# Seven block products for eight: the Delta half of an output projection, by pairs of chunks

## The chip, the cores and the metric

The kernel runs on one core of a Trainium2 chip. The metric is the device time of one execution in microseconds (us), lower being better. Beside the runs' times there is one profiled execution, from which every row of a profile in this document comes.

## The reference

One layer of an encoder: RMSNorm, one input projection, two head groups that read it (a bidirectional gated DeltaNet of 4 heads of 128, and windowed attention of 8 heads of 64), and one output projection of both groups' outputs, added to the input. Cut to what matters here, with S = 2048 rows and D = 1024 columns:

```python
dn = dn * jax.nn.silu(dn_z)          # (2048, 512): 4 heads x 128
sw = sw * jax.nn.silu(sw_z)          # (2048, 512)
mix = jnp.concatenate([dn, sw], axis=-1)
x = x + mix @ w_out                  # w_out: (1024, 1024)
```

The "Delta half" of the output is `dn @ w_out[:512]`.

## The kernel before, in words

The rows are 16 chunks of 128. Phase A (`phase_a`) normalises, projects and computes the attention group; phase B (`phase_b`) does the delta rule for one head after the other, and the output projection in two halves. The TensorE (PE) multiplies float32 numbers in the type float32r, with each operand split into a high part (a copy to float32r by ScalarE, ACT) and a low part (the rest, by VectorE, DVE); a product is then three matmuls: high x high, low x high, high x low.

*Per head* phase B does `pre_front` (Gram matrices of a chunk, with decays, into tiles `ma`, L703), `solve` and `invert` (the inverse of a triangular block, tiles `pi`, L772) and `scan` (L798): 16 steps forward and 16 backward, each a chain of small matmuls (pk, py, po), DVE updates (r, S) and ACT copies (y, yk). `post` (L855) is called at step 12 for the groups of chunks 4 to 11 and after the last step for the others: it takes squares (jko) and a power on GpSimd (POOL, sso), scales, transposes (tro), multiplies by the gate (zt) and stores to `mix_dn` in DRAM (L882). The scan of one head overlaps the preparation of the next; heads alternate between two pools of tiles, hd0 (heads 0 and 2) and hd1 (heads 1 and 3). Pool kx holds half of head 2's ks and vs.

*The attention half of the output* is 32 units (`sw_units`, L567; a chunk and 512 columns each; tiles mxs, mhs, mls, pcs) that add their product to the input rows (xrs) and store partial rows `part` in DRAM (L603). They fill PE during scans; their staging tiles are in pool swp, their PSUM banks are those of ps_t and ps_g.

*The Delta half* is what the change touches. `load_wo` (L537) loads w_out[:512] as eight pieces of 128x512 and splits each (L545, L546) into pool op; then `out_dn` (L919) is called for the chunks in the order 7, 8, 6, 9, ... 0, 15. It loads 128 rows of `mix_dn` as one 128x512 tile mxd (L922), splits it (mhd L553, mld L554), and `out_half` (L549) computes for each of two halves of the columns 4 x 3 matmuls into a bank pcd (L561 to L563), adds the partial row xrd (loaded by L558, added by L564) and stores it (L565). The chunks 4 to 11 can go ahead once head 3's scan has passed step 12; the others wait for its end.

*Pools.* hd0 and rp, hd1, swp, kx stand on two sides of SBUF. q1, qa, qb (of `pre_front`, `solve` and `invert`), kx, swp and the PSUM pools ps_t, ps_g, ps_i are released together (`pre_stack.close()`, L913); op and ps_c (L914, L915) then take space that they had.

*The order of the work* is not that of the program. `set_order` (L938) builds the graph of all instructions, gives each a cost (L1091; a DMA also a fixed 2.4 us until it lands, L931), plans forward and backward with queues per engine (`plan`, L1174), keeps the plan with the earliest end, and fixes it as the order of each engine and of the DMA queue on SP. In this graph a pool that lies where released pools were waits as a whole: all users of the old pools come before all users of the new one (`behind`, L1045, L1071). Instructions of DVE and POOL with two inputs in SBUF are planned one at a time (L1145, L1215). At run time an instruction waits only for the tiles that it uses, but in this order.

Of the kernel before, what the change touches and what calls it, by code (L numbers as in the profile page):

```python
# [7 lines left out]
F32 = mybir.dt.float32  # L8
F32R = mybir.dt.float32r
AF = mybir.ActivationFunctionType  # L10
ALU = mybir.AluOpType
AX = mybir.AxisListType
PSUM = bass.MemoryType.PSUM
DRAM = bass.MemoryType.DRAM

P = 128
S = 2048
D = 1024
# [4 lines left out]
NQ = 8  # L23
EPS = 1e-6
NDEC = 1
SCRATCH = 1024
NEG = -1e30
FILLF = ((0, 0, 0, 8), (0, 0, 0, 8), (0, 0, 0, 8))
# [4 lines left out]
def tile_hybrid(ctx, tc, t, out, dbg=None):  # L33
# [26 lines left out]
    with ExitStack() as cb, ExitStack() as wide:  # L60
        with ExitStack() as ca:
            consts, late = phase_a(ca, wide, tc, t, ident, nw, bd, gp, mix_sw, kq_d, v_d, zdn_d, zsw_d, dp)
        phase_b(cb, wide, late, tc, t, ident, consts, hp, mix_dn, mix_sw, kq_d, v_d, zdn_d, zsw_d, dp, out)
# [367 lines left out]
def delta_setup(tc, t, ident, bd, gp, ap, bp, pj, q_pool):  # L431
# [71 lines left out]
    dec_d = {}  # L503
    for h in range(NDEC):
        for d in range(2):
# [14 lines left out]
def phase_b(ctx, wide, late, tc, t, ident, consts, hp, mix_dn, mix_sw, kq_d, v_d, zdn_d, zsw_d, dp, out):  # L520
    nc = tc.nc
    V, A, G, T = nc.vector, nc.scalar, nc.gpsimd, nc.tensor
    dma = nc.sync.dma_start

    def pool(name, bufs=1, stack=ctx, **kw):
        return stack.enter_context(tc.tile_pool(name=name, bufs=bufs, reuse_waits="tile", **kw))
# [7 lines left out]

    part_d = [dp.tile([P, D], F32, tag=f"part{c}", name=f"part{c}") for c in range(NCH)]

    def load_wo(pool, k0, name, tg=""):  # L537
        wh = pool.tile([P, 4, D], F32R, tag="woh" + tg, name=f"woh{name}", bufs=1)
        wl = pool.tile([P, 4, D], F32R, tag="wol" + tg, name=f"wol{name}", bufs=1)
        for k in range(4):  # L540
            for j in range(2):
                ns = slice(j * 512, (j + 1) * 512)
                sw = pool.tile([P, 512], F32, tag="ws", name=f"wos{name}_{k}_{j}")
                dma(sw, t["wout"][:, k0 + k, ns])
                A.activation(wh[:, k, ns], sw, AF.Copy)  # L545
                V.tensor_tensor(wl[:, k, ns], sw, wh[:, k, ns].bitcast(F32), ALU.subtract)  # L546
        return wh, wl

    def out_half(pool, bank, w, mx, src, dst, name, nb):  # L549
        wh, wl = w  # L550
        mh = pool.tile([P, 4, P], F32R, tag="mh", name=f"mh{name}", bufs=nb)
        ml = pool.tile([P, 4, P], F32R, tag="ml", name=f"ml{name}", bufs=nb)
        A.activation(mh, mx, AF.Copy)  # L553
        V.tensor_tensor(ml, mx, mh.bitcast(F32), ALU.subtract)  # L554
        for j in range(2):
            ns = slice(j * 512, (j + 1) * 512)
            xr = pool.tile([P, 512], F32, tag="ws", name=f"xr{name}_{j}")
            dma(xr, src[:, ns])  # L558
            ps = bank(j, f"pc{name}_{j}")
            for k in range(4):  # L560
                T.matmul(ps, mh[:, k], wh[:, k, ns], start=(k == 0), stop=False)  # L561
                T.matmul(ps, ml[:, k], wh[:, k, ns], start=False, stop=False)  # L562
                T.matmul(ps, mh[:, k], wl[:, k, ns], start=False, stop=(k == 3))  # L563
            V.tensor_tensor(xr, xr, ps, ALU.add)  # L564
            dma(dst[:, ns], xr)  # L565

    def sw_units(pool):  # L567
        w = {}

# [44 lines left out]
    ORD = (7, 8, 6, 9, 5, 10, 4, 11, 3, 12, 2, 13, 1, 14, 0, 15)  # L614
    pre_stack = ctx.enter_context(ExitStack())
    hd = [pool("hd0")]
    q1 = pool("q1", stack=pre_stack)
    qa = pool("qa", stack=pre_stack)
    qb = pool("qb", stack=pre_stack)
    ps_i = [pool("ps_i0", stack=pre_stack, space=PSUM), pool("ps_i1", stack=pre_stack, space=PSUM)]  # L620
# [16 lines left out]
    def pre_front(h):  # L637
# [12 lines left out]
        for n, c4 in enumerate(FRONT):  # L650
# [7 lines left out]
            for d in range(2):  # L658
                gm = q1.tile([P, 4, P], F32, tag="gm", name=f"dc{h}_{c4}_{d}", bufs=4)
                if h < NDEC:  # L660
                    dma(gm.rearrange("p c i -> p (c i)"), dec_d[h, d][c4])
# [28 lines left out]
            for c2 in range(2):  # L690
# [6 lines left out]
                for k in range(2):  # L697
                    c = 2 * c2 + k
                    cc = 4 * c4 + c
                    for d in range(2):  # L700
                        if h >= NDEC:
                            A.activation(gms[d][:, c], gms[d][:, c], AF.Exp, bias=ngc[:, d, cc, h : h + 1])
# [181 lines left out]
    def bank(k):  # L884
        return lambda nm: (ps_t, ps_g, ps_i[0], ps_i[1])[k].tile([P, 512], F32, tag=("tr", "gh", "inv", "inv")[k], name=nm)
# [13 lines left out]
    with tc.using_default_side("right"):  # L899
# [3 lines left out]
        kx = pool("kx", stack=pre_stack)  # L903
# [6 lines left out]
        invert(h + 1, H)  # L910
    for k in range(32):
        fill(1, bank(k % 2))
    pre_stack.close()  # L913
    op = pool("op", 4)  # L914
    ps_c = pool("ps_c", 4, space=PSUM)  # L915
    with tc.high_priority(-1000000):
        w = load_wo(op, 0, "d")

    def out_dn(c):  # L919
        sc = slice(c * P, (c + 1) * P)  # L920
        mx = op.tile([P, 4, P], F32, tag="mx", name=f"mxd{c}", bufs=2)
        dma(mx, mix_dn[:, :, sc].rearrange("f p s -> p f s"))  # L922
        out_half(op, lambda j, nm: ps_c.tile([P, 512], F32, tag="pc", name=nm), w, mx, part_d[c], out[sc, :], f"d{c}", 2)

    scan(3, H)
    for c in ORD:
        out_dn(c)


ENGINES = ("PE", "DVE", "Activation", "Pool", "SP")  # L930
# [3 lines left out]

SBUF_BYTES = 229344 - SCRATCH - 128

# [372 lines left out]
```

## Time and profile before

| | |
|---|---|
| median of 3 runs | 1280.27 us |
| lowest, highest | 1278.16, 1280.57 us |
| the profiled execution | 1274.25 us |
| its span, first to last instruction | 1272.5 us |
| mean granted PE clock | 0.992 |
| matmuls of the Delta half (pcd) | 384, from 1175.5 us of the span on |
| matmuls of the attention half (pcs) | 384, from 808.1 to 1171.4 us |
| DMA queue of hardware, whole span | 203.92 MB, 52.7% of 16 engines |

Rows of a profile name a line of the kernel (L561), an engine (PE matmuls, PEld weight loads, DVE, ACT, POOL, SPq the DMA queue), an operation, tiles without their numbers (out<-in), and a count (x48). "idle before <- releaser" is time that the engine sat idle, and what ended it. Matmuls are pipelined: the duration of one is longer than the distance to the next. A row of stretches gives from:to, the length, then busy time and count of PE, PEld, DVE, ACT, POOL, then the granted PE clock (1 is full), the DMA engines' busy share, and GB/s.

### The profile page before, as it was taken

How to read it: one execution, taken by the hardware profiler on the slowest of the kernel's cores; microseconds unless marked ns; L12 is line 12 of the kernel's file. 1: busy time of each engine (PE TensorE's matmuls, PEld its weight loads, DVE VectorE, ACT ScalarE, POOL GpSimd, SP SyncE). 2: the span in 40 equal slices, each digit the busy share in tenths (PEclk: the TensorE clock that was granted, in tenths of full speed). 3: DMA queues.
4: the chain of work that ended last, by engine and by line, in shares of the span. 5: the costliest groups of instructions: out<-in, count | busy, mean ns of one | idle time of the engine just before them, and what ended most of it. 6: DMA issues, size and time to landing. Idle time of an engine off the chain costs nothing.

```text
span 1272.5 us, 22253 instructions
## 1 busy us (share of the span) xinstructions
PE 1219.4 (96%) x7066; PEld 1044.4 (82%) x7066; DVE 889.5 (70%) x2154; ACT 703.2 (55%) x2105; POOL 507.4 (40%) x893
## 2 busy tenths in 40 slices
PE   6999999999999999999999998998799899999998
PEld 6998877788889998787788787887688789798876
DVE  4422387999975589999986573788488879557333
ACT  6321254776644677776654425858557955566210
POOL 1330044666613398665221306613672651641000
PEclk9999999999999999999999998999899999999999
DMA  8442254322544434522137826967965974746675
GB/s 269 145 132 76 95 180 128 97 97 81 180 132 144 130 96 116 158 87 67 58 117 244 224 96 189 276 189 207 270 169 154 269 191 138 217 145 214 227 242 205
DMA packets 225510, 205.34 MB, mean 161 GB/s; under 512 B 48497, under 2 KB 175089, under 8 KB 225393
## 3 DMA queue, kind: packets, MB, share of 16 engines
q1 hardware_dynamic: 225392, 203.92, 52.7%
q8 instruction: 56, 0.92, 0.3%
q14 instruction: 62, 0.50, 0.1%
HBM read 138.79 MB, written 65.08 MB: 160 GB/s over the span
## 4 chain that ended last, share of the span: by engine, by line
PE 67%; DVE 12%; DMA 9%; ACT 7%; issue 3%; POOL 1%; SPq 0%; DVEq 0%; ACTq 0%; POOLq 0%
PE pf_c L191 4%; PE pf_c L192 4%; PE pf_c L193 4%; PE pf_z L191 4%; PE pf_z L192 4%; PE pf_z L193 4%; PE pi L772 4%; DVE acc L242 3%; PE pt L363 3%; PE pq_q L202 2%; PE pq_q L204 2%; PE pq_q L203 2%; PE pcd L561 2%; PE pcd L563 2%; PE pcd L562 2%
## 5 line engine op out<-in xcount | busy, mean ns | idle before, releaser
L191 PE MATMUL pf_c<-xhi,wh_c 128*128 128x512 f32 x384 | 151.0, 404 | 0.7 <-DVE acc L242 0.4
L192 PE MATMUL pf_c<-xlo,wh_c 128*128 128x512 f32 x384 | 150.6, 401 | 0.0
L193 PE MATMUL pf_c<-xhi,wl_c 128*128 128x512 f32 x384 | 149.1, 401 | 0.0
L242 DVE SCALAR_TENSOR_TENSOR acc<-pf_c,cw,acc 128x512 f32<-128x512 f32 (+1 forms) x192 | 140.3, 743 | 11.3 <-ACT acc L238 9.2
L358 POOL TENSOR_SCALAR pr<-pr,st 128x384 f32<-128x384 f32 (+1 forms) x128 | 80.1, 648 | 71.3 <-DVE st L356 60.0
L191 PE MATMUL pf_z<-xhi,wh_z 128*128 128x512 f32 x256 | 86.6, 401 | 0.5 <-DVE zo L215 0.5
L349 ACT ACTIVATE pr<-pr,st 128x384 f32<-128x384 f32 (+1 forms) x128 | 76.1, 596 | 19.6 <-DVE st L345 19.1
L192 PE MATMUL pf_z<-xlo,wh_z 128*128 128x512 f32 x256 | 86.2, 399 | 0.0
L191 PEld LDWEIGHTS pf_c<-xhi,wh_c 128*128 128x128 f32 x384 | 72.1, 188 | 15.3 <-DVE acc L242 1.7
L193 PE MATMUL pf_z<-xhi,wl_z 128*128 128x512 f32 x256 | 84.7, 397 | 0.0
L192 PEld LDWEIGHTS pf_c<-xlo,wh_c 128*128 128x128 f32 x384 | 72.3, 188 | 13.0
L193 PEld LDWEIGHTS pf_c<-xhi,wl_c 128*128 128x128 f32 x384 | 71.8, 188 | 13.0
L345 DVE CUSTOM_DVE_ANT_0 pr<-s,mask,sink 128x384 f32<-128x384 f32 (+1 forms) x128 | 72.5, 593 | 12.4 <-PE s L344 8.3
L367 ACT ACTIVATE ph<-pt 128x512 fp32r<-128x512 f32 x92 | 53.0, 596 | 40.9 <-PE pt L363 39.1
L826 ACT ACTIVATE yk<-py,ck 128x128 f32<-128x128 f32 x120 | 43.9, 366 | 49.5 <-PE py L821 48.4
L363 PE MATMUL pt<-ident,pr 128*128 128x128 f32 x368 | 67.2, 274 | 1.9 <-DVE q L327 1.1
L368 DVE TENSOR_TENSOR pl<-pt,ph 128x512 fp32r<-128x512 f32 x92 | 61.6, 681 | 5.1 <-ACT ph L367 5.0
L703 DVE SCALAR_TENSOR_TENSOR ma<-gh,bp,dc 128x256 f32<-128x256 f32 x128 | 54.9, 476 | 10.4 <-PE gh L694 8.7
L363 PEld LDWEIGHTS pt<-ident,pr 128*128 128x128 f32 x368 | 46.5, 140 | 17.7 <-DVE pl L368 3.0
L202 PE MATMUL pq_q<-wh_q,xhi 128*128 128x256 f32 x256 | 60.3, 285 | 0.6 <-ACT sgkv L261 0.3
L599 PE MATMUL pcs<-wohs,mhs 128*128 128x512 f32 x128 | 57.7, 451 | 2.9 <-ACT mhs L593 2.3
L814 DVE SCALAR_TENSOR_TENSOR r<-pk,negc,vs 128x128 f32<-128x128 f32 x120 | 41.5, 346 | 27.1 <-PE pk L812 26.6
(251 smaller groups left out, 3709.8 us busy)
## 6 DMA issues: line engine op xcount, KB each, us to landing
kqc<-kq_d SPq DMA_DIRECT2D x120, 128.0 KB, 3.0
ws_c<-wt SPq DMA_DIRECT2D x48, 256.0 KB, 3.3
xr<-x SPq DMA_DIRECT2D x16, 512.0 KB, 6.3
ws_z<-wt SPq DMA_DIRECT2D x32, 256.0 KB, 3.9
kq<-kq_d SPq DMA_DIRECT2D x16, 512.0 KB, 5.3
m_d<-ma SPq DMA_DIRECT2D x32, 256.0 KB, 5.4
mxs<-mix_sw SPq DMA_DIRECT2D x32, 256.0 KB, 3.8
xrs<-x SPq DMA_DIRECT2D x32, 256.0 KB, 3.6
```

What stands on the lines that cost most here:

```text
L191: T.matmul(ps, hi[:, k, cs], xhi[b][:, k], start=(k == 0), stop=False)
L192: T.matmul(ps, hi[:, k, cs], xlo[b][:, k], start=False, stop=False)
L193: T.matmul(ps, lo[:, k, cs], xhi[b][:, k], start=False, stop=(k == KC - 1))
L202: T.matmul(ps[:, :n], xh, hi[:, k, :n], start=(k == 0), stop=False)
L242: V.scalar_tensor_tensor(av, ps[:, lo:], cw[:, i, k : k + 1], av, ALU.mult, ALU.add)
L345: V.tensor_tensor_reduce(pr[j][:, :n], ps[:, :n], mask[:, lo * P : hi * P], 1.0, sink[:, hh : hh + 1], ALU.add, ALU.min, accum_out=nm[:, j ...
L349: A.activation(pr[j][:, :n], pr[j][:, :n], AF.Exp, bias=nm[:, j : j + 1], scale=-1.0, accum_out=den[:, j : j + 1])
L358: G.tensor_scalar(pr[j][:, :n], pr[j][:, :n], den[:, j : j + 1], 1.0, ALU.mult, ALU.mult)
L363: T.transpose(pt[:, j], pr[j][:, (kb - lo) * P : (kb - lo + 1) * P], ident)
L368: V.tensor_tensor(pl, ptf, ph.bitcast(F32), ALU.subtract)
L599: T.matmul(ps, mh[:, k], wh[:, k], start=(k == 0), stop=False)
L703: V.scalar_tensor_tensor(ma[d, c4][:, c], gh[:, k], bp[:, d, cc : cc + 1], gms[d][:, c : c + 1].to_broadcast([P, 2, P]), ALU.mult, ALU.mult,)
```

## The change

The 16 chunks are taken as 8 pairs (7, 8), (6, 9), ... (0, 15). For a pair, the two chunks' 512 inputs are a 2 x 2 matrix of blocks a (row: chunk c or e; column: heads 0 and 1, or heads 2 and 3), and the weights a 2 x 2 matrix b (row: the same heads; column: 512 output columns each). The product is formed from seven block products in place of eight: a11 b11, a12 b21, a12' b22, a22 b21', a21+a22 by b12-b11, and two more, where the marked ones are sums of several blocks. GpSimd makes the sums of a (four per pair) and, once, those of b (four for each of the two 128-row parts of a block).

Seven split weights take 56 KB per partition in place of 32. They are made in tiles that came free: hd0's ma and two of its ks, and q1's kq, gm and vt, with the unsplit blocks staged in kx; q1 is no longer released. Pool op holds only what a pair needs; ps_c has four banks: two for the first accumulator (pa), which takes products 0, 5, 6 and 3 one after the other with reads between, and two that alternate between product 1 and products 4 and 2 (pc). The pass that orders the instructions is unchanged.

The diff's core (removed: `load_wo`, `out_half`, `out_dn` and their calls, which stand above):

```diff
+WSB = 7
+MXB = 8
+U2B = 2
...
-    q1 = pool("q1", stack=pre_stack)
+    q1 = pool("q1")
...
+    wh, wl = [], []
+    for p in range(4):
+        w = spare(hd[0], [P, 2, 2, 512], f"ma{p}", f"wod{p}")
+        wh.append([w[:, 0, k] for k in range(2)])
+        wl.append([w[:, 1, k] for k in range(2)])
...
+    with tc.high_priority(-1000000):
+        for k in range(2):
+            B = []
+            for n, (r, j) in enumerate(((0, 0), (2, 0), (2, 1), (0, 1))):
+                B.append(kx.tile(flat, F32, tag=("ks0", "vs0", "ks1", "vs1")[n], name=f"wos{k}_{n}", bufs=1))
+                dma(B[n], t["wout"][:, r + k, j * 512 : (j + 1) * 512])
+            b11, b21, b22, b12 = B
+            for p in (0, 4, 2, 6, 5, 1, 3):
+                if p == 4:
+                    G.tensor_tensor(b11, b12, b11, ALU.subtract)
+                elif p == 6:
+                    G.tensor_tensor(b12, b22, b12, ALU.subtract)
+                elif p == 5:
+                    G.tensor_tensor(b22, b22, b11, ALU.subtract)
+                elif p == 3:
+                    G.tensor_tensor(b21, b21, b22, ALU.subtract)
+                a = (b11, b21, b22, b21, b11, b22, b12)[p]
+                A.activation(wh[p][k], a, AF.Copy)
+                V.tensor_tensor(wl[p][k], a, wh[p][k].bitcast(F32), ALU.subtract)
     pre_stack.close()
-    op = pool("op", 4)
-    ps_c = pool("ps_c", 4, space=PSUM)
+    op = pool("op", 1)
+    ps_c = pool("ps_c", 2, space=PSUM)
+
+    def out_pair(c, e):
...
+        mx = {}
+        for k in range(2):
+            for x in (c, e):
+                mx[x, k] = op.tile([P, 2, P], F32, tag="mx", name=f"mxd{x}_{k}", bufs=MXB)
+                dma(mx[x, k], mix_dn[2 * k : 2 * k + 2, :, x * P : (x + 1) * P].rearrange("f p s -> p f s"))
+        a11, a12, a21, a22 = mx[c, 0], mx[c, 1], mx[e, 0], mx[e, 1]
...
+        f = {2: S4[:, 3], 4: S4[:, 0], 5: S4[:, 1], 6: S4[:, 2]}
+        G.tensor_tensor(f[6], a11, a21, ALU.subtract)
+        G.tensor_tensor(f[4], a21, a22, ALU.add)
+        G.tensor_tensor(f[5], f[4], a11, ALU.subtract)
+        G.tensor_tensor(f[2], a12, f[5], ALU.subtract)
+        for hi, lo, x in (
+            (xh[0], xl[0], a11), (xh[1], xl[1], a12), (xh[3], xl[3], a22),
+            (bh[:, 3:6], bl[:, 3:6], S4[:, 0:3]), (xh[2], xl[2], f[2]),
+        ):
+            A.activation(hi, x, AF.Copy)
+            V.tensor_tensor(lo, x, hi.bitcast(F32), ALU.subtract)
+
+        def prod(ps, p, first):
+            for k in range(2):
+                on = dict(skip_group_check=not first)
+                T.matmul(ps, xh[p][:, k], wh[p][k], start=first and k == 0, stop=False, **on)
+                T.matmul(ps, xl[p][:, k], wh[p][k], start=False, stop=False, **on)
+                T.matmul(ps, xh[p][:, k], wl[p][k], start=False, stop=k == 1, **on)
...
+        o11 = row(c, 0)
+        prod(p1, 0, True)
+        V.tensor_tensor(o11, o11, p1, ALU.add)
+        prod(p2, 1, True)
+        V.tensor_tensor(o11, o11, p2, ALU.add)
+        put(c, 0, o11)
+        prod(p5, 4, True)
+        o22 = row(e, 1)
+        V.tensor_tensor(o22, o22, p5, ALU.add)
+        prod(p1, 5, False)
+        u2 = op.tile([P, 512], F32, tag="u2", name=f"u{nm}", bufs=U2B)
+        A.activation(u2, p1, AF.Copy)
+        prod(p5, 2, False)
+        o12 = row(c, 1)
+        V.tensor_tensor(o12, o12, p5, ALU.add)
+        G.tensor_tensor(o12, o12, u2, ALU.add)
+        put(c, 1, o12)
+        prod(p1, 6, False)
+        V.tensor_tensor(o22, o22, p1, ALU.add)
+        put(e, 1, o22)
+        prod(p1, 3, False)
+        o21 = row(e, 0)
+        V.tensor_tensor(o21, o21, p1, ALU.add)
+        put(e, 0, o21)
 
     scan(3, H)
-    for c in ORD:
-        out_dn(c)
+    for c, e in zip(ORD[::2], ORD[1::2]):
+        out_pair(c, e)
```

`row` loads 128x512 of `part` into one of seven buffers (tag ws), `put` stores it to the output; mh0 and ml0 (product 0's splits), the tile of the six others and the sums have two buffers each, mx eight.

More of the change, by code (lines that the diff above doesn't have):

```diff
@@ L535, in phase_b @@
     part_d = [dp.tile([P, D], F32, tag=f"part{c}", name=f"part{c}") for c in range(NCH)]
[L537 to L565, printed above, removed]
     def sw_units(pool):
@@ L912, in phase_b @@
         fill(1, bank(k % 2))
-    pre_stack.close()
-    op = pool("op", 4)
-    ps_c = pool("ps_c", 4, space=PSUM)
[L916 to L923, printed above, removed]
+    pair = [P, 2, 512]
@@ new lines, in phase_b, with spare @@
+    flat = [P, 512]
+    def spare(p, shape, tag, name, bufs=1):
+        return p.tile(shape, F32R, tag=tag, name=name, bufs=bufs)
+    wh, wl = [], []
[3 more added lines that the diff above has]
+        wl.append([w[:, 1, k] for k in range(2)])
+    w = [spare(q1, pair, "kq", f"wod4_{x}", 2) for x in range(2)]
+    wh.append([w[0][:, k] for k in range(2)])
+    wl.append([w[1][:, k] for k in range(2)])
@@ new lines, in phase_b @@
+    w = [spare(q1, flat, "gm", f"wod5_{x}", 4) for x in range(4)]
+    wh.append(w[:2])
+    wl.append(w[2:])
+    wh.append([spare(q1, flat, "vt", f"wod6_{k}", 2) for k in range(2)])
+    wl.append([spare(hd[0], flat, f"ks{k}", f"wod6_{2 + k}") for k in range(2)])
+    with tc.high_priority(-1000000):
[17 more added lines that the diff above has]
+                V.tensor_tensor(wl[p][k], a, wh[p][k].bitcast(F32), ALU.subtract)
@@ new lines, in phase_b, with row, put @@
+    pre_stack.close()
+    op = pool("op", 1)
+    ps_c = pool("ps_c", 2, space=PSUM)
+    def out_pair(c, e):
+        nm = f"d{c}"
+        mx = {}
[4 more added lines that the diff above has]
+        a11, a12, a21, a22 = mx[c, 0], mx[c, 1], mx[e, 0], mx[e, 1]
+        xh = [op.tile([P, 2, P], F32R, tag="mh0", name=f"mh0{nm}", bufs=2)]
+        xl = [op.tile([P, 2, P], F32R, tag="ml0", name=f"ml0{nm}", bufs=2)]
+        bh = op.tile([P, 6, 2, P], F32R, tag="mh", name=f"mh{nm}", bufs=2)
+        bl = op.tile([P, 6, 2, P], F32R, tag="ml", name=f"ml{nm}", bufs=2)
+        xh += [bh[:, k] for k in range(6)]
+        xl += [bl[:, k] for k in range(6)]
+        S4 = op.tile([P, 4, 2, P], F32, tag="sm", name=f"sm{nm}", bufs=2)
+        f = {2: S4[:, 3], 4: S4[:, 0], 5: S4[:, 1], 6: S4[:, 2]}
[15 more added lines that the diff above has]
+                T.matmul(ps, xh[p][:, k], wl[p][k], start=False, stop=k == 1, **on)
+        def row(x, j):
+            xr = op.tile([P, 512], F32, tag="ws", name=f"xrd{x}_{j}", bufs=WSB)
+            dma(xr, part_d[x][:, j * 512 : (j + 1) * 512])
+            return xr
+        def put(x, j, o):
+            dma(out[x * P : (x + 1) * P, j * 512 : (j + 1) * 512], o)
+        p1, p2, p5 = (ps_c.tile([P, 512], F32, tag="pc" if k else "pa", name=f"pc{nm}_{k}") for k in range(3))
+        o11 = row(c, 0)
[22 more added lines that the diff above has]
+        put(e, 0, o21)
```

## The prediction, made before the changed kernel was run

> **What bounds the kernel now.** I read the page first, for the span and for the engine that is nearly always busy, and then stretches of the end, since the change touches nothing ahead of the last scan's second half but the making of its weights.
>
> ```profile
> span 1272.5 us, 22253 instructions
> PE 1219.4 (96%) x7066; PEld 1044.4 (82%) x7066; DVE 889.5 (70%) x2154; ACT 703.2 (55%) x2105; POOL 507.4 (40%) x893
> ```
>
> The profiled execution took 1274.25 us, 1.75 us more than its span. A busy PE is not PE at its peak, so the stage itself must be read. First its instructions (the tile pcd, the product of the output half in question), then busy time in stretches, where "(x48)" counts instructions:
>
> ```profile
> L561 PE MATMUL pcd<-wohd,mhd x128: 388/389/501, 1175.5 to 1268.0; 128*128 128x512 f32 x128
> L563 PE MATMUL pcd<-wold,mhd x128: 388/389/398, 1176.8 to 1268.4; 128*128 128x512 f32 x128
> ```
> ```profile
> 1223.70:1235.15 11.45, 11.18 (x48) 8.91 (x48) 2.56 (x5) 1.00 0.65 229
> ```
> ```profile
> 1226.11 1.07 PE L561 MATMUL pcd<-wohd,mhd 128*128 128x512 f32 x4
> 1227.02 1.07 PE L562 MATMUL pcd<-wohd,mld 128*128 128x512 f32 x4
> 1227.92 1.07 PE L563 MATMUL pcd<-wold,mhd 128*128 128x512 f32 x4
> ```
>
> Three lines of 128 matmuls fill the stretch from 1175.5 to 1268.8 us. One matmul is in flight 389 ns, but eight of them start between 1226.11 and 1227.92: one every 1.81 / 8 = 0.226 us. That is the price of a matmul here. Two chunks (48 matmuls, the second fence) take 11.45 us, of which 48 x 0.226 = 10.85 is matmul and 0.60 is lost. So PE bounds this stage at 95%, at a granted clock of 1.00. DMA engines are busy 0.65 of it, and the other engines less than half:
>
> ```profile
> 1097.00:1125.00 28.00, 26.02 (x191) 23.20 (x190) 12.77 (x37) 19.87 (x74) 22.34 (x61) 1.00 0.61 176
> 1125.00:1160.00 35.00, 35.00 (x269) 32.84 (x268) 19.42 (x62) 20.45 (x71) 5.22 (x8) 1.00 0.50 145
> 1175.00:1180.00 5.00, 4.93 (x25) 3.80 (x23) 3.01 (x8) 1.96 (x6) 0.00 (x0) 1.00 1.00 345
> 1223.70:1258.11 34.41, 33.60 (x145) 26.74 (x145) 11.06 (x19) 3.80 (x6) 0.00 (x0) 1.00 0.68 230
> ```
>
> The columns after the length are PE, weight loads, DVE, ACT and POOL, then the clock, the DMA share and GB/s.
>
> **The change part by part.** *Matmuls.* Per pair of chunks the old code issues 2 x 2 x 4 x 3 = 48, the new one 7 products x 2 x 3 = 42. Over 8 pairs 48 go: 48 x 0.226 = **-10.85 us**. Their form is the same (a 128x128 block held, 512 columns streamed), so I keep the price.
>
> *Loss per pair in the steady stage.* A pair now has 42 x 0.226 = 9.5 us of PE. For the other engines I take these durations:
>
> ```profile
> L381 POOL TENSOR_TENSOR ot<-ot,zc x16: 733/740/1227, 230.9 to 476.6; 128x256 f32<-128x256 f32 x16
> ```
> ```profile
> L590 POOL TENSOR_TENSOR mxs<-mxs,zcs x16: 1266/1272/1447, 860.4 to 1163.3; 128x512 f32<-128x512 f32 x16
> ```
> ```profile
> L310 ACT ACTIVATE k<-ptk 128x256 fp32r<-128x256 f32 x16 | 6.0, 377 | 5.1 <-PE ptk L308 5.0
> L553 ACT ACTIVATE mhd<-mxd 128x512 fp32r<-128x512 f32 x16 | 10.1, 633 | 62.7 <-PE pcd L563 60.1 <-DMA mxd<-mix_dn 2.6
> L167 ACT ACTIVATE xhi<-xt 128x1024 fp32r<-128x1024 f32 x12 | 12.5, 1055 | 2.3 <-DVE xt L166 2.3
> L311 DVE TENSOR_TENSOR k<-ptk,k 128x256 fp32r<-128x256 f32 x16 | 6.6, 414 | 0.1
> L554 DVE TENSOR_TENSOR mld<-mxd,mhd 128x512 fp32r<-128x512 f32 x16 | 10.9, 684 | 2.0 <-ACT mhd L553 2.0
> L168 DVE TENSOR_TENSOR xlo<-xt,xhi 128x1024 fp32r<-128x1024 f32 x12 | 14.7, 1262 | 0.0
> L564 DVE TENSOR_TENSOR xrd<-xrd,pcd 128x512 f32<-128x512 f32 x32 | 20.6, 683 | 54.0 <-PE pcd L563 54.0
> ```
>
> No row has a 768-wide split; between 512 and 1024 I estimate 0.84 us on ACT and 0.97 on DVE. Then per pair POOL has 4 x 0.74 + 1.27 = 4.2 us, ACT 4 x 0.38 + 0.84 + 0.63 = 3.0, and DVE 6 x 0.68 + 4 x 0.41 + 0.97 = 6.7. All three fit under 9.5, so none becomes the bound by its load alone. What can cost is order. The new code reads an accumulator and then goes on adding to it: the first bank after products 0, 5 and 6, the third after product 4. Behind 0, 4 and 5 other products of the pair stand (1.36 us each, 6 x 0.226), as long as a read takes. Only product 3 must follow product 6 directly. Uncovered, that costs the drain of the last matmul (0.39 - 0.23) plus the read of 0.68, some 0.9 us with hand-offs; covered by the next pair's products, nothing. The splits of the next pair, which cost the 0.60 now, have their sums ready ahead (eight mx tiles, two sets of sums), and product 0 has a tile of its own. Bounds for the new loss per pair: 0 to 0.9. I take 0.60, the loss of today's row, so the term is **0** with bounds of -4.8 and +2.4 over 8 pairs.
>
> *The hand-over into the stage.* The chain of waits (first two rows: the DMAs) and the order of the SP queue and PE show how the stage starts:
>
> ```profile
> 1170.10 4.87 DMA mix_dn<-zt
> 1174.98 4.78 DMA mxd<-mix_dn
> ```
> ```profile
> 1171.36 0.40 PE L601 MATMUL pcs<-wols,mhs 128*128 128x512 f32 x1
> 1175.55 0.71 PE L561 MATMUL pcd<-wohd,mhd 128*128 128x512 f32 x2
> ```
> ```profile
> 1165.87 0.33 SPq L882 DMA_DIRECT2D mix_dn<-zt  x1
> 1169.59 0.42 SPq L922 DMA_DIRECT2D mxd<-mix_dn  x1
> 1172.70 0.33 SPq L603 DMA_DIRECT2D part<-xrs  x1
> ```
>
> Today the first chunk is loaded at 1169.59, before the other half's last unit (pcs) is stored at 1172.70. By the sizes in the code, pool op ends at 109 KB per partition and pool swp begins at 113 KB. With q1 kept and op at 63 KB, op now reaches 141 KB, over swp and kx. The ordering pass puts all of a pool's users behind all users of what it overlaps (its gates for released pools), so SP gets the first mx loads behind that store; the loads themselves need only their own tiles. Last pcs matmul 1171.8, add and store issue 1172.7, load 4.8, ACT 0.38, DVE 0.41: first product at about 1178.3 in place of 1175.5, +2.8. In that gap PE has the scan's last steps, which it would otherwise run later; they need DVE and ACT between their matmuls and fill part of it. The pair also needs chunk 8: loaded at 1174.98 today, 1179.8 landed; then three POOL sums (2.2) and the wide split (1.8) make product 4 ready at 1183.8. Until then PE has products 0 and 1 of two pairs, 24 x 0.226 = 5.4 us from 1178.3. Bounds: 0 (the pass pulls pcs or the scan's norm forward) to +9 (it waits for the store to land as its model does, 4.7 us more, and nothing fills). I take **+2.5**, nearest to the 2.8 of the rows.
>
> *Weights.* Eight loads stay. ACT and DVE splits go from 8 to 14 each, and POOL gets 8 differences. They leave the stretch from 1167 to 1178 for one from about 1097, where the last matmul of the third scan has read hd0's ma:
>
> ```profile
> 1096.81 0.38 PE L839 MATMUL po<-y,ma 128*128 128x128 f32 x2
> ```
> ```profile
> L545 ACT ACTIVATE wohd<-wosd x8: 625/632/646, 1167.2 to 1177.1; 128x512 fp32r<-128x512 f32 x8
> L546 DVE TENSOR_TENSOR wold<-wosd,wohd x8: 682/687/694, 1167.9 to 1177.8; 128x512 fp32r<-128x512 f32 x8
> ```
>
> 14 x 0.63 = 8.8 us on ACT, 14 x 0.69 = 9.6 on DVE, 8 x 1.27 = 10.2 on POOL, into 63 us in which ACT is idle 23 us, DVE 31 and POOL 35 (the first two window rows above). PE hides it there, being full with the last inverse, pcs and the scan; without that cover it would cost at most the longest, 10.2. ACT and DVE get 5.1 and 5.5 us free at the hand-over. I take 0, bounds -1 and +3.
>
> *The end.* Today four adds run together after the last products; afterwards the last add follows product 3, which waits for the read of product 6 unless the last two pairs are interleaved: 0 to +0.9, I take **+0.4**.
>
> Sum: -10.85 + 0 + 2.5 + 0 + 0.4 = -7.95. Against the profiled execution 1274.25 that is 1266.3. The runs shown have a median of 1280.27, 6.0 above it, so I forecast 1280.27 - 7.95 = **1272.3 us**.
>
> **The rivals.** *A, slower: reads of the accumulators queue behind splits.* DVE takes its work in order. If product 6's read stands behind the next pair's wide split and a narrow one (0.97 + 0.41), the 0.9 becomes 2.3 us per pair, in the place of 0.6: 8 x 1.7 = +13.6, and with the rest +5.6: 1285.9. It decides from 0.6 + 7.95 / 8 = 1.6 us of loss per pair. For it: today's DVE does three adds in a row before the split that PE waits for. Against it: the order already interleaves four products (runs of four on a line above), and there are two first banks.
>
> *B, no change: transfers set the pace.* A pair still moves what two chunks move, 229 GB/s x 11.45 = 2.62 MB; in 10.1 us that is 260 GB/s. Seven row buffers serve four rows a pair, each held through a load and a store. If the pace stays 11.45, the 8 x 1.35 us are lost again: 1272.3 + 10.8 = 1283.1; if half the pairs wait, 1277.7, and three quarters give the no-change case, 1280.4. Against it: 345 GB/s at a share of 1.00 in the row from 1175 on.
>
> *C, the hand-over at its upper bound:* +9 in place of +2.5, 1278.8. There the clock joins in:
>
> ```profile
> 920.00:925.00 5.00, 2.06 (x18) 1.85 (x17) 1.53 (x4) 1.16 (x5) 2.36 (x5) 1.00 0.85 178
> 925.00:930.00 5.00, 5.00 (x31) 4.96 (x31) 1.99 (x5) 2.29 (x9) 3.06 (x6) 0.66 0.82 193
> ```
>
> Behind 5 us with PE busy for 2.06, the granted clock is 0.66 for the next 5: 1.7 us lost. A gap of 9 us without filling would add that once: 1280.5. The Trainium skill ("TensorE: Matmul & The Clock Gate", section "What's actually happening") says that an idle window of about 3.4 us halves the PE clock and a busy one restores it; by it, a hand-over with such a gap costs an estimated 1.7 us more, and the rows just shown agree in size. The scan's steps make a gap that long unlikely.
>
> *D, the better case:* loss per pair 0 and no hand-over cost: 1280.27 - 10.85 - 4.8 + 0.4 = 1265.0.
>
> *E, the change doesn't do what it says,* for instance if matmuls that continue a read bank run slower than 0.226: 336 x 0.01 = 3.4 us for each 0.01; no row shows one, and I count it with B.
>
> **How the numbers follow.** Forecast 0.50 (1268 to 1277.5); D 0.10; C 0.12; B and E 0.12; A 0.16. The range reaches from D's 1265 to 1284, past B's full price and short of A's: about 0.8 inside. A measurement of this kernel can tell about 0.2%, 2.6 us, from no change. Faster by more than that (below 1277.7): forecast and D, plus half of C and of B's milder part, 0.70. Within: 0.10. Slower: A and the rest of B, 0.20.
>
> **What would show it.** Right: 336 matmuls of 128x512 in the last stage, 0.226 us apart, 42 in 9.5 to 10.4 us; PE at 1.00; the stage shorter by 8 us, all of it after 1175. First product near 1178. Weight splits between 1100 and 1165 with no new PE idle there. Wrong: more than 1.6 us lost per pair with PE waiting for DVE adds on the first bank (A); PE or POOL waiting for DMA with a share near 1.00 (B); a start after 1182 or a clock under 1.00 behind it (C); or PE idle, or a later end of the inverse, between 1097 and 1165, which I cost at nothing.

## The result and the profile after

| | before | after |
|---|---|---|
| median of the runs beside each other (4 and 4) | 1280.42 us | 1269.93 us |
| ratio, 95% interval | | 0.9926 [0.9905, 0.9946] |
| profiled execution, its span | 1274.25, 1272.5 us | 1270.95, 1268.8 us |
| first pi matmul (inverses of phase B) | 774.7 us | 777.5 us |
| first and last pcd matmul | 1175.5, 1268.4 us | 1183.0, 1264.8 us |

The forecast was 1272.3 us, the time is 1269.93. Of the 10.5 us between the medians the two profiled executions show only 3.3: that of before is a fast one among runs of 1274 to 1284 us. The order of every engine is the same in both kernels up to 739 us, where that of DVE parts first (POOL's at 772, PE's and ACT's behind 780). By then after is already 2.6 us behind before, so 2.6 of the 2.8 us by which the inverses start later are no work of the change. Of the traces, only stretches behind them are compared below.

The page of after, its second and fourth line:

```profile
span 1268.8 us, 22319 instructions
...
PE 1213.9 (96%) x7018; PEld 1036.2 (82%) x7018; DVE 918.6 (72%) x2200; ACT 716.8 (56%) x2143; POOL 562.6 (44%) x941
```

48 matmuls are gone, and POOL, DVE and ACT have more to do. Now the stage of after, first by instructions of pcd (first and last start stand before the semicolon), then by the start of some matmuls:

```profile
L958 PE MATMUL pcd<-wod,mh0d x16: 388/389/495, 1183.0 to 1251.9; 128*128 128x512 f32 x16
L960 PE MATMUL pcd<-wod,mhd x96: 388/389/482, 1186.6 to 1264.8; 128*128 128x512 f32 x96
```
```profile
1174.99 0.39 PE L796 MATMUL po<-S,kqc 128*128 128x128 f32 x2
1175.21 0.39 PE L803 MATMUL po<-yk,ks 128*128 128x128 f32 x2
...
1207.51 0.39 PE L959 MATMUL pcd<-wod,mld 128*128 128x512 f32 x1
1207.74 0.39 PE L960 MATMUL pcd<-wod,mhd 128*128 128x512 f32 x1
```

Two 128-column matmuls take 0.22 us from start to start, one of 512 columns 0.23: prices of 0.113 and 0.226 us, the second as before (1.81 / 8, unrounded below). So the work in a stretch can be counted, and what is left of its length is **lost**. First before, then after, in stretches (PE is the first pair behind the length):

```profile
1165.00:1195.00 30.00, 28.79 (x146) 23.17 (x146) 18.15 (x42) 10.79 (x28) 0.00 (x0) 1.00 0.73 237
1195.00:1230.00 35.00, 34.73 (x160) 28.55 (x159) 13.17 (x24) 8.87 (x31) 1.64 (x1) 1.00 0.70 234
1230.00:1268.65 38.65, 37.84 (x164) 30.07 (x162) 12.89 (x21) 3.80 (x6) 0.00 (x0) 1.00 0.61 207
```
```profile
1165.00:1195.00 30.00, 27.33 (x155) 21.39 (x154) 22.43 (x57) 19.63 (x78) 11.66 (x13) 1.00 0.66 203
1195.00:1230.00 35.00, 35.00 (x156) 28.42 (x155) 26.29 (x44) 9.90 (x22) 16.55 (x19) 1.00 0.80 262
1230.00:1265.05 35.05, 33.74 (x148) 27.17 (x146) 20.25 (x34) 6.24 (x13) 10.96 (x11) 1.00 0.66 218
```

Of before's matmuls in the three rows 89, 146 and 164 have 512 columns and the others 128, of after's 51, 153 and 148. Lost are 30 - 89 x 0.226 - 57 x 0.113 = 3.4, then 0.4 and 1.5 in before, and 6.7, 0.0 and 1.6 in after: 5.3 against 8.3 us. The change gives back 3.0 us in its stage, nearly all of it at the hand-over.

What set the hand-over, in the order of the SP queue in after:

```profile
1173.53 0.32 SPq L576 DMA_DIRECT2D part<-xrs  x1
1174.80 1.49 SPq L855 DMA_DIRECT2D mix_dn<-zt  x2
1176.38 0.88 SPq L964 DMA_DIRECT2D xrd<-part  x2
1177.31 4.25 SPq L934 DMA_DIRECT2D mxd<-mix_dn  x8
```

The first chunks of `mix_dn` are stored at 1174.80, not at 1165.87 as before: that store, and not only the partial row ahead of it, now holds the loads. The inverse ends at 1165.9 instead of 1158.2, and the scan's step 12 and its `post` come later. In return the scan's last steps run ahead of the stage, the second `post` (sso) at 1187.00 instead of 1204.77. That is why a start 7.5 us later costs PE only 3.3.

What PE waits for between 1160 and the end of after:

```profile
PE pcd L958 <- DVE xrd L973: 1.3, 1, 1.3
PE pcd L959 <- DVE ml0d L953: 1.1, 1, 1.1
PE pcd L958 <- ACT mhd L952: 0.6, 1, 0.6
```

The second and third are the start of the stage. The first is one stop at 1234, whose cause stands in the chain of waits:

```profile
1223.50 3.85 DMA out<-xrd
...
1227.37 0.37 SPq L964
...
1228.30 5.62 DMA xrd<-part
...
1234.05 0.70 DVE xrd L973
...
1234.79 0.50 PE pcd L958
```

A row buffer is stored, only then loaded again, and the first bank (L973) cannot be read until the row is there. None of the seven buffers was free.

### The profile page after: what moved, and what is told of

Read it like the earlier page. It is cut to its first block, busy times and chain, and to the rows that moved or that the text cites. A ratio compares the mean times of both kernels' runs of the same rounds, so it can differ in the third digit from the quotient of the medians.

```text
span 1268.8 us, 22319 instructions
## 1 busy us (share of the span) xinstructions
PE 1213.9 (96%) x7018; PEld 1036.2 (82%) x7018; DVE 918.6 (72%) x2200; ACT 716.8 (56%) x2143; POOL 562.6 (44%) x941
## 4 chain that ended last, share of the span: by engine, by line
PE 66%; DVE 11%; DMA 9%; ACT 8%; POOL 2%; issue 2%; SPq 1%; DVEq 0%; ACTq 0%; POOLq 0%
PE pf_c L194 4%; PE pf_c L195 4%; PE pf_c L196 4%; PE pf_z L194 4%; PE pf_z L195 4%; PE pf_z L196 4%; PE pi L745 3%; DVE acc L245 3%; PE pt L366 3%; DMA xr<-x 3%; PE pq_q L205 2%; PE pq_q L207 2%; PE pq_q L206 2%; PE pcd L958 2%; PE pcd L960 2%
## 5 line engine op out<-in xcount | busy, mean ns | idle before, releaser
L348 DVE CUSTOM_DVE_ANT_0 pr<-s,mask,sink 128x384 f32<-128x384 f32 (+1 forms) x128 | 72.5, 593 | 12.5 <-PE s L347 8.1
L206 PE MATMUL pq_q<-wh_q,xlo 128*128 128x256 f32 x256 | 60.6, 284 | 0.0
```

What stands on the lines that cost most here:

```text
L206: T.matmul(ps[:, :n], xl, hi[:, k, :n], start=False, stop=False)
L348: V.tensor_tensor_reduce(pr[j][:, :n], ps[:, :n], mask[:, lo * P : hi * P], 1.0, sink[:, hh : hh + 1], ALU.add, ALU.min, accum_out=nm[:, j ...
```

## The experiments

My **theory** after the result: the matmuls give about 10.85 us in the stage; interleaved products cover the reads of the accumulators; the hand-over gives back some 2 to 3; the weights cost nothing. **Rivals**: the gain is due to the new order of the rest and not to the missing products; the weights' work holds up the last scan; the row buffers set the pace. "Order kept" means that the instructions keep the order planned for after (or for e3, in e5), with added ones next to their originals; "planned anew" means that the ordering pass made a new order. Ratios are to the kernel before, with 95% intervals.

### e0_again: after, unchanged

> The changed kernel as it is, once more, so that the others have their own yardstick on the same chip. By the prediction's terms 0.62% faster than the kernel before; the four runs already seen gave 0.74% with an interval from 0.54 to 0.95%, the two profiled executions only 3.3 us. I expect a ratio of 0.992 to 0.995.

1270.89 us, 0.9932 [0.9910, 0.9955]. The gain is there again. From the first pi to the last pcd matmul it took 488.4 us in the trace (after 487.3, before 493.7).

### e1_eight: eight products in the new order

Product 1 is formed twice in each pair; order kept.

```diff
-        prod(p2, 1, True)
+        more = prod(p2, 1, True)
+        TWICE[prod(p2, 1, True)[0]] = more
```

> The changed kernel with product 1 formed twice per pair (the second time from a cleared bank), 48 matmuls more, every other instruction in the same order. If PE sets the pace of the stage (the prediction's main term), each matmul costs its 0.226 us: 10.8 us more than the changed kernel, and so level with the kernel before, within 3 us. If transfers and row buffers set the pace (rival B), the added matmuls lie in time that PE waits anyway: 0 to 4 us more.

1278.91 us, 1.0001 [0.9981, 1.0022], 8.0 above e0_again.

```profile
L960 PE MATMUL pcd<-wod,mh0d x16: 389/389/502, 1181.4 to 1258.1; 128*128 128x512 f32 x16
...
L962 PE MATMUL pcd<-wod,mhd x112: 388/389/485, 1185.0 to 1272.3; 128*128 128x512 f32 x112
```

The stage starts as early as after's and takes 90.9 us between these starts instead of 81.8: 9.1 for 48 matmuls, where 10.85 is their price; the rest fell into places where PE waited anyway. With the 48 matmuls back the time is that of before, to within the interval's 3 us. So under this order the gain over before is these matmuls, and all other parts of the change come to nothing in sum.

### e2_rows8: eight row buffers

Order kept: the plan is made as if there were seven.

```diff
-WSB = 7
+WSB = 8
...
-            home[f"{tag}_{name}_{p.id}"] = (name, m.bufs)
+            home[f"{tag}_{name}_{p.id}"] = (name, 7 if (tag, name) == ("ws", "op") else m.bufs)
```

> The changed kernel with eight row buffers in place of seven, and the order of all queues kept. The profile after shows one place in the stage where PE stops, 1.3 us near 1234, for an add whose row was loaded late. If the buffer is what held that load, 1.0 to 1.5 us less; if the place in the DMA queue holds it (the load stands behind stores that wait for adds), 0 to 0.3 us less; if rows set the pace in general (rival B), 3 us less or more.

1269.60 us, 0.9924 [0.9903, 0.9945]: 1.3 under e0_again, which the intervals cannot tell from nothing. The trace can: the same list of waits of PE begins

```profile
PE pcd L959 <- DVE ml0d L953: 1.1, 1, 1.1
PE pcd L958 <- ACT mhd L952: 0.7, 1, 0.7
```

and has no L973 any more. The stop at 1234 was the row buffers'.

### e3_gate: op's tiles ordered behind what they overlap, tile by tile

The pass no longer puts pool op as a whole behind swp and kx; planned anew.

```diff
+        if name == "op":
+            at = spans[name][1]
+            for tag, m in pools[name].tag_meta.items():
+                to = at + -(-m.max_size_bytes // P // 32) * 32 * m.bufs
+                over = [o for o in olds if spans[o][1] < to and at < spans[o][2]]
...
+                gate([k for o in over for k in users.get(o, [])], mine)
+                at = to
+            continue
```

> The changed kernel, with the ordering pass holding back only those tiles of pool op that lie over the released pools, and not the pool as a whole, so that mx, mh0 and ml0 no longer wait for the attention half's last store. The pass orders anew. If that hold makes the hand-over's cost (2.5 us in the prediction), 1.5 to 3 us less than the changed kernel and a first product 2 us or more ahead; if the norm's chain and two DMA trips set the start, less than 1 us either way.

1267.29 us, 0.9906 [0.9882, 0.9931], 3.6 under e0_again.

```profile
L958 PE MATMUL pcd<-wod,mh0d x16: 389/389/478, 1179.8 to 1247.7; 128*128 128x512 f32 x16
```

The first product comes 3.2 us earlier. It is the only replanned kernel that gained, and e10 below shows how far a new order can move the time by itself. In its trace the hand-over (1165 to 1195) loses 4.5 us instead of after's 6.7; 2.4 us less are lost between 980 and 1060 too, where the gate holds nothing. So the gate is a likely cause of some 2 us, and not a shown one.

### e5_gate_rows8: both

e3's order, kept, with eight row buffers.

> The kernel of e3_gate in its own order, with eight row buffers in place of seven. In e3_gate PE still stops once, 1.2 us near 1229, for an add that waits for its row. If the two costs are separate, 0.8 to 1.3 us below e3_gate, so a ratio to the kernel before of about 0.990; if the row buffer's stop only moves, no change against e3_gate.

1267.90 us, 0.9897 [0.9875, 0.9919]: beside e3's 0.9906 no difference that can be measured, and the best ratio of all. PE's wait for L973 falls from 1.5 us in e3 to 0.4.

### e6_strict: products not interleaved

The pcd matmuls in the order of the program, pair after pair; planned anew.

```diff
+    turn = [7, 6, 5, 4, 3, 2, 1, 0]
+    mine = [sorted({k for x in used if x.startswith(f"pcd{c}_") for k in used[x] if insts[k][1] == "PE"}) for c in turn]
+    for a, b in zip(mine, mine[1:]):
+        gate(a, b)
+    for a in mine:
+        for i, j in zip(a, a[1:]):
+            edge(i, j)
```

> The changed kernel with the stage's matmuls held in program order: pair after pair, products 0, 1, 4, 5, 2, 6, 3 each in one piece, so that nothing stands between product 6 and product 3 while the bank is read. The ordering pass plans all else anew. By the prediction 0.9 us per pair is uncovered then: 7 us more than the changed kernel, which takes most of the gain. By rival A, where reads queue behind splits on DVE, 2.3 us per pair: 14 to 18 us more, slower than the kernel before. If the reads cost nothing in any order, 0 to 2 us more.

1280.56 us, 1.0015 [0.9998, 1.0033]. The stage starts at 1185.0 us and takes 91.3 between first and last start, 9.5 more than after's. The place where product 3 must follow the read of product 6, in the timeline, and that wait in the list of PE's waits:

```profile
1230.60 0.39 PE L960 MATMUL pcd<-wod,mhd 128*128 128x512 f32 x1
1231.03 0.69 DVE L989 TENSOR_TENSOR xrd<-xrd,pcd 128x512 f32<-128x512 f32 x1 [0.67 <-PE pcd L960]
...
1231.77 0.50 PE L958 MATMUL pcd<-wod,mhd 128*128 128x512 f32 x1 [0.78 <-DVE xrd L989]
```
```profile
PE pcd L958 <- DVE xrd L989: 5.5, 7, 0.8
```

Two matmuls stand 1.17 us apart instead of 0.226: an uncovered read costs **0.94 us**. Seven such waits, 6.6 us, are most of the 9.5. So it is the interleaving that makes the change pay: without it the stage takes about as long as before's (91.3 us, before 92.9 between first and last start). That the time lands on that of before as well holds for this plan.

### e4_twice and e8_planned: the weights' splits done twice

14 splits more on ACT (8.8 us) and on DVE (9.7): in e8 planned anew (the edit shown), in e4 the same with the order kept.

```diff
-                A.activation(wh[p][k], a, AF.Copy)
-                V.tensor_tensor(wl[p][k], a, wh[p][k].bitcast(F32), ALU.subtract)
+                for _ in range(2):
+                    A.activation(wh[p][k], a, AF.Copy)
+                for _ in range(2):
+                    V.tensor_tensor(wl[p][k], a, wh[p][k].bitcast(F32), ALU.subtract)
```

> The changed kernel with each of the 14 ACT copies and 14 DVE rests that split the weights done twice, one right behind the other, all queues otherwise in the same order: 8.8 us more on ACT and 9.6 on DVE between about 1092 and 1152. The prediction has this work at nothing, hidden by PE (bounds -1 and +3): then 0 to 1 us more than the changed kernel. If the early weights are what costs ahead of the stage, 3 us more or above.

> The changed kernel with the weights' 14 copies on ACT and 14 rests on DVE done twice, as in e4_twice, but known to the ordering pass, which plans all anew. In e4_twice, where the queues kept an order made for half of this work, it cost 7.8 us. If the work is hidden when it is planned for (the prediction's term of nothing, bounds -1 and +3), 0 to 3 us more than the changed kernel; if ACT and DVE have no room ahead of the stage, 6 us more or above again.

e4: 1278.22 us, 0.9993 [0.9978, 1.0007], some 8 over after, where hidden work was to cost 0 to 1. In its stretches PE has holes where after has none (22.29 of 25 us, 11.94 of 15; after's 1125:1160 has 34.95 of 35):

```profile
1125.00:1150.00 25.00, 22.29 (x166) 19.76 (x165) 18.03 (x42) 20.99 (x60) 19.19 (x30) 1.00 0.52 155
1150.00:1165.00 15.00, 11.94 (x85) 10.33 (x84) 14.16 (x29) 11.36 (x31) 4.46 (x4) 1.00 0.36 103
```

Under them PE waits for r, S and yk of the scan, and in the timeline of DVE these stand behind splits:

```profile
1156.41 2.93 DVE L925 TENSOR_TENSOR wod<-wos,wod 128x512 fp32r<-128x512 f32 x2
1159.27 0.34 DVE L788 SCALAR_TENSOR_TENSOR r<-pk,negc,vs 128x128 f32<-128x128 f32 x1
```

PE waits 1.37 us for that r. e8: 1284.88 us, 1.0048 [1.0027, 1.0069], some 14 over after, where 6 or more was to mean that ACT and DVE have no room. But its first pi matmul already comes at 787.0, 9.5 us late and some 300 us ahead of the first split, and from there to the last pcd matmul it takes 490.9, only 3.6 over after. With the order fixed, there is no slack for the double work; a plan that knows of it seems to find room for most, which one trace of one new order does not show for certain.

### e9_oneblock: the weights' work left out

Only product 0's weights are split, and all seven products use them, so the output is not the reference's; 12 of 14 splits and all 8 differences go. Planned anew.

```diff
+    wh, wl = [wh[0]] * 7, [wl[0]] * 7
...
-            for p in (0, 4, 2, 6, 5, 1, 3):
+            for p in (0,):
```

> The changed kernel with the splits of one block instead of seven: it leaves out 12 of the 14 splits and all 8 differences and uses the first block's weights for all products, so its output is not the reference's. Planned anew. If the weights' work is hidden, 0 to 1 us less than the changed kernel; if it costs ahead of the stage what e4_twice suggests for a unit of it, 5 us less or more.

1270.71 us, 0.9935 [0.9911, 0.9959]; 488.3 us from first pi to last pcd (after 487.3, e0_again 488.4). Without the weights' work nothing is gained here; but the order is a new one (its hand-over loses 10.5 us instead of 6.7), so a cost of a few us could hide behind it. The two rows of that work in after:

```profile
L922 ACT ACTIVATE wod<-wos x14: 617/630/641, 1092.7 to 1148.9; 128x512 fp32r<-128x512 f32 x14
L923 DVE TENSOR_TENSOR wod<-wos,wod x14: 674/693/1370, 1093.4 to 1151.8; 128x512 fp32r<-128x512 f32 x14
```

### e7_late: the weights loaded behind the last inverse

```diff
+    last = [k for x in used if x.startswith("pi4_3_3_") for k in used[x]]
+    wos = [k for x in used if x.startswith(("wos0_", "wos1_")) for k in used[x]]
+    gate(last, wos)
```

> The changed kernel with the loads of the weights held back until the last triangular inverse is done (about 1157 to 1166), where the kernel before made its weights. The ordering pass plans all else anew. The chain of loads, 14 splits and 8 differences takes some 30 us there and stands ahead of the first pairs: if early weights matter to the gain, 5 us more or above; if the place is free to choose, 0 to 2 us more.

1275.08 us, 0.9972 [0.9957, 0.9986], some 5 over after; the first product at 1187.3. From first pi to last pcd 490.1, 2.8 over after. Planned anew, so the split between the late weights and the order is not shown.

### e10_replan and e11_before61: another order for the same two kernels

One constant in the pass, the planned cost of an ACT instruction, is 61 ns instead of 60: in after (e10) and in before (e11). No instruction changes, only the order.

```diff
-            return 60 + 0.86 * m + 85 * (scalars > 0) + 110 * (len(o) > 1) + 100 * short
+            return 61 + 0.86 * m + 85 * (scalars > 0) + 110 * (len(o) > 1) + 100 * short
```

> The changed kernel with one constant of the ordering pass moved by 1 ns (an ACT instruction's fixed cost, 61 in place of 60), nothing else: the pass then finds another order. It shows how much a new order alone moves the time, which bounds what can be read from the kernels that were planned anew. I expect 0 to 2 us either way; if 4 us or more, differences of that size between planned kernels say nothing of their edits.

> The kernel before, with the one constant of the ordering pass that e10_replan changed in the changed kernel (60 to 61 ns in the planned cost of an ACT instruction). It pairs with e10_replan (1281.04 us, 1.0014 of before; from the first matmul of the inverses, pi, to the last of the stage, pcd, 490.8 us in its trace; before 493.7, after 487.3). Both plans differ from their parents early in the program, so the question is whether seven products beat eight also under this other constant. Theory (the gain is the change's own, and the constant costs both kernels something ahead of phase B by chance): e11 is 5 to 12 us above e10_replan, 1286 to 1293 us, and its length from the first pi to the last pcd matmul is 494 to 503 us, at least 3 above e10_replan's. Rival (the gain of the changed kernel came in good part from the order that the pass happened to find): e11 is level with before or better, 1274 to 1282 us, and within 3 us of e10_replan, with the same length from first pi to last pcd within 3 us. In between (1282 to 1286): part of each. The stage itself, first to last pcd matmul, should in any case be 8 to 12 us longer than e10_replan's 86.4.

e10: 1281.04 us, 1.0014 [0.9997, 1.0031]. e11: 1278.44 us, 1.0001 [0.9983, 1.0018]. **With this constant seven products are no faster than eight.** The theory wanted e11 5 to 12 us above e10, the rival wanted both level. In time they are (e11 2.6 us below), but from first pi to last pcd e11 is 4.7 us shorter, more than the rival's 3, and its stage (first to last pcd start) is 5.8 us longer than e10's (92.2 and 86.4), not the 8 to 12 that were to hold in any case. The four kernels from first pi to last pcd matmul (its start + 0.23), "lost" counted as above (the 256-column matmuls of the Gram matrices, gh, at the 0.216 us from start to start that they take in after):

| | before | after | e11 (eight) | e10 (seven) |
|---|---|---|---|---|
| first pi matmul, us | 774.7 | 777.5 | 785.1 | 785.4 |
| length to the last pcd, us | 494.0 | 487.5 | 486.4 | 491.0 |
| matmul work, us | 429.4 | 418.5 | 429.4 | 418.5 |
| lost, us | 64.6 | 69.0 | 57.0 | 72.5 |
| of it 980 to 1060 | 9.6 | 13.6 | 7.7 | 15.3 |
| 1060 to 1165 | 10.0 | 6.8 | 5.6 | 5.7 |
| 1165 to 1195 | 3.4 | 6.7 | 4.3 | 6.9 |
| 1195 to the end | 1.9 | 1.6 | 1.8 | 7.2 |

The 10.85 us of matmul are saved both times. From e11 to e10, 15.5 us are lost again. In e10 (its clock is the third number from the end of a row):

```profile
980.00:1060.00 80.00, 72.74 (x467) 62.92 (x466) 58.00 (x182) 54.97 (x227) 40.38 (x85) 0.94 0.72 212
...
1240.60:1243.30 2.70, 0.01 (x1) 0.00 (x0) 0.69 (x1) 0.00 (x0) 0.00 (x0) 0.87 0.97 324
1243.30:1249.40 6.10, 6.06 (x14) 4.79 (x15) 2.83 (x4) 0.90 (x2) 5.64 (x7) 0.50 0.48 165
1249.40:1256.00 6.60, 6.60 (x30) 5.42 (x29) 2.69 (x5) 1.89 (x5) 0.82 (x2) 1.00 0.72 225
```
```profile
1232.29 5.63 DMA out<-xrd
...
1237.94 4.53 DMA xrd<-part
...
1242.59 0.70 DVE xrd L973
```
```profile
PE pcd L958 <- DVE xrd L973: 3.8, 2, 2.7
```

and in e11:

```profile
980.00:1060.00 80.00, 76.65 (x536) 68.66 (x536) 67.87 (x208) 59.70 (x245) 39.48 (x90) 1.00 0.76 223
```

Three places make up nearly all of the 15.5. In the stage 5.4: the row buffers stop PE twice, for 1.0 and 2.7 us (the second and third fence: store, load, read, as at 1234 in after), and behind the second stop the granted clock is 0.50 for 6.1 us, in which 14 matmuls start where the next row has 30 in 6.6. At the hand-over 2.6, the price that the prediction gave. And 7.6 between 980 and 1060, where no instruction of the change runs (the weights' loads begin at 1089.6): there e10's granted clock is 0.94 on average (80 x 0.06 = 4.8 us), e11's 1.00. The drop comes at 1013.9, behind 3.4 us (from 1010.5) in which PE was busy for 1.16. The stage's 5.4 and the hand-over's 2.6 belong to the change; of the 7.6, whether the clock's share comes back in other executions of e10 stays open. The rest is no accident of one execution: counted the same way, five traces of after's order (after, e0, e1, e2, e4) lose 12.2 to 13.8 us between 980 and 1060, all twelve traces of the changed kernel and of what was made from it 9.9 to 15.3, and before and e11 9.6 and 7.7. So each of the twelve lost more than both of those in a stretch that the change does not touch, in the closest case by 0.3 us. Why is not shown, and no run tests it. Eight row buffers under e10's order, the test of the 5.4, were not tried.

## Why the prediction was right, point by point

- *Matmuls, -10.85.* Right: the price stayed 0.226 us, 48 are gone, and putting 48 back costs 8.0 us of time and 9.1 of the stage (e1). Rival E is refuted: banks that were read and added to again are no slower (the median distance of the stage's matmuls in after is 0.227 us).
- *Loss per pair, 0 by interleaving, 0.9 uncovered.* Right on both ends: 1.6 us lost in after from 1195 on against before's 1.9, and 0.94 us for an uncovered read (e6). The 1.6 and 1.9 are 0.2 to 0.3 us a pair, under the 0.60 that the prediction read from one stretch. Rival A is refuted: PE never waits for L989 in after's stage, and in e6 for 0.8 us at most, which the read itself takes up.
- *Hand-over, +2.5.* The size was near (3.3), the step only half right. The loads do stand behind the partial row's store, but the store of `mix_dn`, 8.9 us later than before, stands behind it again. The prediction took the scan's time as given; the new order moved it. The first product came at 1183.0 and not near 1178, past the 1182 set as the sign of C; C's price did not follow, since the scan's last steps filled the gap and the clock stayed at 1.00.
- *Weights, 0.* Nothing speaks against it, and no run shows it to the us. Between 1060 and 1165 after loses 6.8 us, before 10.0 and e11 5.6, and leaving the work out gained nothing (e9, with a new order). The end of the inverse came 7.7 us later all the same, which the prediction named as a sign against itself; PE had other work in that time (between 1130 and 1165 a count of 31 matmuls of 512 columns and 242 of 128 leaves 0.6 us lost; before, 35 and 220, 2.2). That there is no slack for twice the work in this order (e4) is new.
- *The end, +0.4, and the sum.* From 1165 on 3.0 us are given back; the terms there say 2.5 + 0 + 0.4 = 2.9. With -10.85 that makes -7.9; the medians differ by 10.5 (by 8.8 in the runs beside e0), e1 and e0 by 8.0. From first pi to last pcd the traces differ by 6.5. Outside the stage after loses 4.0 us more than before between 980 and 1060 and 3.2 less between 1060 and 1165: that the two nearly cancel is luck, since the prediction had no term for either.
- *Rival B* had 0.12 with E and was refuted for a steady pace, but its mechanism is there: one stop of 1.3 us in after, and two with a drop of the clock in e10, 5.4 us in all. The prediction's row of DMA share could not show it, since buffers ran out and not bandwidth.
- *What the prediction did not see:* that it compares two orders. It said that the change touches nothing ahead of the last scan's second half but the weights, and so took the pass's new order, which differs from 739 us on, to be as good as the old one outside the stage. e10 and e11 show that a nanosecond in a planned cost can move a kernel by as much as the change does: after's time by 10 us, and before's phase B by 7.6 (494.0 to 486.4), though not its time (1.0001), since phase B began 10.4 us later. The forecast was right in its terms for the stage, and in its time by luck of the order that the pass happened to find; 10.85 us less of PE work has no certain sign in this kernel's time.

## What to carry to other kernels

Count what an engine's work is worth apart from what its order loses: work removed from a full PE stays removed, but the loss around it is redrawn with each plan. Where a pass orders the program, test a change also with the order kept and with one planned cost shifted by a trifle, ahead of calling a per cent its own. An accumulator that is read and then added to again cost nothing here where other products stood behind the read, and 0.94 us each time where none did.

## What the runs showed of the hardware

- The clock falls after less idle time than I had thought, and stays low well behind the stop. In e10 PE's last matmul before the stop ends at 1240.60; by 1243.30 the mean clock of those 2.70 us is 0.87, so it was at half for some 0.7 of them, then 0.50 for 6.1 us under a PE that was busy 6.06 of it: about 3 us lost behind a stop of 2.7. The Trainium skill ("TensorE: Matmul & The Clock Gate", section "What's actually happening") gives half rate after an idle window of about 3.4 us and full rate after a busy one of the same length, in windows that run freely; half rate agrees, and the fall here came after some 2 us of idling. The stop of 1.3 us in after, at 1234, left the clock at 1.00.
- The same program had its drops in other places in its two traces. After has 0.50 from 900 to 905, where e0_again, its twin, has 1.00 and is at 0.66 only in the next row; from 845 to 850 it is 1.00 in after and 0.74 in e0_again. First after, then e0_again:

```profile
900.00:905.00 5.00, 4.68 (x11) 3.74 (x12) 1.31 (x7) 3.37 (x21) 1.35 (x1) 0.50 1.00 331
905.00:910.00 5.00, 3.99 (x15) 2.60 (x15) 2.99 (x6) 2.97 (x9) 2.26 (x7) 0.88 0.81 180
```
```profile
900.00:905.00 5.00, 1.65 (x8) 1.03 (x6) 2.46 (x11) 2.45 (x10) 2.23 (x2) 1.00 1.08 303
905.00:910.00 5.00, 4.80 (x14) 3.31 (x12) 0.82 (x3) 2.34 (x16) 1.64 (x1) 0.66 0.93 305
```

- An operation of DVE and one of POOL, each with two inputs in SBUF, nearly run one behind the other here, though both are issued. In after a sum that takes 0.74 us alone is shown with 1.35 and a split of 0.42 with 0.96 where they meet. The first three rows take 1.83 us together; one behind the other, at 0.95, 0.74 and 0.42, they would take 2.11, and the two splits alone 1.37:

```profile
1188.41 0.96 DVE L953 TENSOR_TENSOR mld<-smd,mhd 128x768 fp32r<-128x768 f32 x1
1188.61 1.35 POOL L946 TENSOR_TENSOR smd<-smd,mxd 128x256 f32<-128x256 f32 x1
1189.28 0.96 DVE L953 TENSOR_TENSOR mld<-mxd,mhd 128x256 fp32r<-128x256 f32 x1
...
1193.10 0.74 POOL L944 TENSOR_TENSOR smd<-mxd,mxd 128x256 f32<-128x256 f32 x1 [1.57 <-DVE mld L953]
```
